# Second attention of a two-layer encoder: four units' softmax denominators turned at once, sent through DRAM and applied three units later

## The chip, the cores and the metric

The kernel is one program on one NeuronCore of a Trainium2 chip. The core has TensorE (PE in the profile: matmuls and transposes, results in PSUM), VectorE (DVE), ScalarE (ACT), GpSimd (POOL) and SyncE (SP, which here only issues transfers). Each engine works through its own instructions in order and waits on semaphore counts for what others produce. PSUM has eight banks of 128 partitions by 512 float32 words. The metric is the device time in microseconds of one execution. Before the change it was 1394.36 us, the median of three runs (1393.14 to 1395.08).

## What is computed

The reference is a two-layer encoder on a sequence of 1024 positions with 1024 features in float32. Layer 0 mixes tokens by a dilated window attention, layer 1 by a latent attention with 16 heads of width 64, and each layer ends in a gated residual and a layer norm. The change lies in layer 1's attention:

```python
s = (jnp.einsum('bqhd,bkhd->bhqk', qn, k_nope)
     + jnp.einsum('bqhd,bkd->bhqk', qr, k_rope)).astype(jnp.float32) * scale
p = jax.nn.softmax(s, axis=-1).astype(v.dtype)
return jnp.einsum('bhqk,bkhd->bqhd', p, v)
...
y = o * jax.nn.silu(gate)
return y @ w_out
```

For each head, every query row of 1024 scores is exponentiated and divided by its sum (the denominator), multiplied with the values, and the result is multiplied with a gate. Because the gate multiplies the same rows, the division may be made on the gate instead of on the probabilities, before or after the gate has met the attention output.

## The kernel before

Every float32 operand of a large matmul is split into a high and a low part of type float32r, and three matmuls (high by high, low by high, high by low; lines L89 to L91) replace one.

Layer 1's attention is `layer_b_attention`. It runs over 128 units u: 16 heads times 8 blocks of 128 queries. The parts of a unit are spread over several turns of the loop:

- `front(u)`: six matmuls of 128x512 into a scores tile `s` (two banks, two buffers).
- `soft(u)`: VectorE takes the row maximum (L1251). `expo(u)`: ScalarE's exponential with the row sum as a by-product (L1257).
- `middle(u)`, two turns later: eight PE transposes of the probabilities `pr` (L1270) into two one-bank tiles `t`; ScalarE casts each to the high part `pth` (L1273) and VectorE subtracts for the low part `ptl` (L1274); VectorE takes the reciprocal of the row sum (L1275), GpSimd spreads it over 64 columns of a tile `den` (L1276). The even and the odd unit share the tiles.
- `back(w)`, every second turn, for the pair of units w: one PE transpose of `den` (L1285) into columns 256 to 383 of a one-bank tile `o`; sixteen matmuls of 128x256 into columns 0 to 255 of the same bank (L1293, "the value matmuls" below); two ScalarE copies out of it (L1298, L1299); VectorE multiplies the turned reciprocals with the gate (L1302); GpSimd adds the two halves and multiplies with that product into the gate tile `gT` (L1305, L1306).

The one-bank tiles (`t`, `o`, and `m` of the projections) rotate through four banks; the scores take the other four.

Between the units two generators, `b_turn` and `b_qk`, prepare the queries and keys of the next two heads with the up-projection weights `wuh`/`wul`, which `b_weights` loads (SyncE) and splits (ScalarE L1110, GpSimd L1111), once in 16 units; `b_v` makes the values of four heads once in 32 units.

TensorE and SyncE run in the order in which the code is written. The orders of ScalarE, VectorE and GpSimd are set by a scheduler when the program is built, so for these the place of a line in the code is not its place in the queue; the built program tells it. All three wait in order: an instruction that is not ready holds everything behind it.

## Time and profile before

| | |
|---|---|
| median of three runs | 1394.36 us |
| profiled execution | 1399.57 us, its span 1397.8 us |
| second attention | from 817 to 1308 us of the span |
| PE busy in the span | 1355.3 us (97%) |
| DVE, ACT, POOL busy in the span | 938.9 (67%), 820.3 (59%), 573.6 us (41%) |

A row of a group reads: line, engine, operation, tile written <- tiles read, shape, xcount, then busy time in us and mean ns of one, then the idle time of that engine just before these instructions and what ended it. In a row of a timeline stand start, duration (both us from the span's start), engine, line, operation, shapes; rows next to each other of the same kind are merged with their count. In a row of a table by stretches stand the stretch, its length, the busy time and count of PE, PEld (weight loads), DVE, ACT and POOL, then the granted share of the TensorE clock, the share of the transfer engines and GB/s. PE's busy time is that of pipelined matmuls whose ends are modelled: a matmul shown with 0.28 us starts 0.12 us after the one before.

### The profile page before, as it was taken

Reading aid. Unit: us, or ns where it says so; the run is one execution under the profiler, and the core shown is the slowest. Engines: PE = TensorE matmul, PEld = TensorE weight load, DVE = VectorE, ACT = ScalarE, POOL = GpSimd, SP = SyncE. Lnnn points to the kernel's source line nnn. Section 1 sums busy time; section 2 is a strip of 40 time slices with the busy share of each in tenths; the row PEclk is TensorE's granted clock in tenths of the full one; section 3 lists DMA queues with packets and bytes.
Section 4 is the critical chain, followed back from the end, with each engine's and each line's share of the span. In section 5 each row is a group of like instructions: output and inputs, shape, how many; then the busy total and the mean of one; then the engine's idle time right before and its main releaser. Section 6 shows DMA issues by size and latency. Waiting matters only on the chain.

```text
span 1397.8 us, 21019 instructions
## 1 busy us (share of the span) xinstructions
PE 1355.3 (97%) x7523; PEld 1160.8 (83%) x7523; DVE 938.9 (67%) x1708; ACT 820.3 (59%) x1604; POOL 573.6 (41%) x657
## 2 busy tenths in 40 slices
PE   6999999999999999999999999999999999999897
PEld 5788888888888788888987888888889888898786
DVE  7654354555455492746745178898988889888787
ACT  3575565565443452425752178788787878888321
POOL 5341233132122226903742254634463463444653
PEclk9999999999999999999999999999999999999999
DMA  9422211022244302544145001010010100014132
GB/s 356 112 64 36 59 50 50 25 60 73 95 151 123 99 31 77 180 149 151 61 119 166 21 14 37 16 30 16 22 29 18 35 16 16 16 61 133 49 113 83
DMA packets 39721, 105.26 MB, mean 75 GB/s; under 512 B 5126, under 2 KB 11270, under 8 KB 39617
## 3 DMA queue, kind: packets, MB, share of 16 engines
q1 hardware_dynamic: 35608, 91.80, 21.3%
q0 software_dynamic: 3552, 12.06, 3.5%
q8 instruction: 60, 0.98, 0.3%
q14 instruction: 45, 0.36, 0.1%
q10 hardware_dynamic: 456, 0.05, 0.0%
HBM read 87.60 MB, written 8.43 MB: 69 GB/s over the span
## 4 chain that ended last, share of the span: by engine, by line
PE 74%; DVE 12%; ACT 5%; issue 4%; DMA 4%; SPq 0%; POOL 0%; DVEq 0%; ACTq 0%
PE pj L89 7%; PE pj L91 7%; PE pj L90 7%; PE o L1293 5%; PE t L1270 5%; PE po L89 4%; PE po L91 4%; PE po L90 4%; DVE mb L1251 3%; PE s L91 3%; PE s L89 3%; PE s L90 3%; PE pg L89 2%; PE pg L90 2%; PE pg L91 2%
## 5 line engine op out<-in xcount | busy, mean ns | idle before, releaser
L89 PE MATMUL pj<-uh,wh 128*128 128x512 f32 x528 | 216.0, 409 | 0.0
L91 PE MATMUL pj<-uh,wl 128*128 128x512 f32 x528 | 207.4, 393 | 0.0
L90 PE MATMUL pj<-ul,wh 128*128 128x512 f32 x528 | 207.4, 393 | 0.0
L1274 DVE TENSOR_TENSOR ptl<-t,pth 128x512 fp32r<-128x512 f32 x256 | 165.4, 682 | 3.0 <-ACT pth L1273 0.9
L1251 DVE TENSOR_REDUCE mb<-s 128x1 f32<-128x1024 f32 x128 | 155.8, 1217 | 7.9 <-PE s L91 6.3
L1257 ACT ACTIVATE pr<-s,mb 128x1024 f32<-128x1024 f32 x128 | 143.4, 1120 | 29.2 <-DVE mb L1251 21.1
L1273 ACT CAST pth<-t 128x512 fp32r<-128x512 f32 x256 | 138.9, 589 | 36.2 <-PE t L1270 34.1
L102 POOL TENSOR_TENSOR wl<-wraw,wh 128x1024 fp32r<-128x1024 f32 x43 | 106.6, 2485 | 106.7 <-ACT wh L101 54.6
L1270 PEld LDWEIGHTS t<-ident,pr 128*128 128x128 f32 x1024 | 119.3, 140 | 19.7 <-DVE ptl L1274 2.6
L1270 PE MATMUL t<-ident,pr 128*128 128x128 f32 x1024 | 133.2, 272 | 1.9 <-DVE ptl L1274 1.9
L1293 PE MATMUL o<-pth,vq 128*128 128x256 f32 x512 | 130.4, 292 | 0.0
L1293 PE MATMUL o<-ptl,vq 128*128 128x256 f32 x512 | 125.5, 283 | 0.8 <-DVE ptl L1274 0.8
L507 ACT ACTIVATE sb<-sb,stat 128x256 f32<-128x256 f32 (+1 forms) x144 | 67.0, 467 | 98.6 <-DVE stat L501 98.5
L91 PEld LDWEIGHTS pj<-uh,wl 128*128 128x128 f32 x528 | 99.4, 188 | 22.2
L1276 POOL COPY den<-mb 128x64 f32<-128x64 f32 x128 | 30.1, 236 | 203.2 <-DVE mb L1275 193.6
L90 PEld LDWEIGHTS pj<-ul,wh 128*128 128x128 f32 x528 | 100.1, 190 | 14.3
L89 PEld LDWEIGHTS pj<-uh,wh 128*128 128x128 f32 x528 | 99.9, 189 | 14.5
L89 PE MATMUL s<-kb,q 128*128 128x512 f32 x256 | 104.4, 408 | 0.2 <-ACT pr L1257 0.2
L91 PE MATMUL s<-kb,q 128*128 128x512 f32 x256 | 101.3, 396 | 0.0
L90 PE MATMUL s<-kb,q 128*128 128x512 f32 x256 | 100.8, 394 | 0.0
L1293 PEld LDWEIGHTS o<-ptl,vq 128*128 128x128 f32 x512 | 97.7, 191 | 1.4 <-DVE ptl L1274 1.4
L1293 PEld LDWEIGHTS o<-pth,vq 128*128 128x128 f32 x512 | 97.7, 191 | 0.2
(288 smaller groups left out, 3317.6 us busy)
## 6 DMA issues: line engine op xcount, KB each, us to landing
wraw<-wa SPq DMA_DIRECT2D x36, 512.0 KB, 4.9
ada<-ada_row SPq DMA_DIRECT2D x64, 256.0 KB, 3.6
wraw<-wo_a SPq DMA_DIRECT2D x18, 512.0 KB, 3.6
ada<-ada_ss SPq DMA_DIRECT2D x16, 512.0 KB, 8.2
kb<-kb POOLq DMA_DIRECT2D x30, 256.0 KB, 3.4
xc<-xt SPq DMA_DIRECT2D x8, 512.0 KB, 9.2
xr<-x SPq DMA_DIRECT2D x8, 512.0 KB, 5.7
xn_d<-z POOLq DMA_DIRECT2D x8, 512.0 KB, 4.6
```

What stands on the lines that cost most here:

```text
L89: mm(out, wh, xh, start=start, stop=False)
L90: mm(out, wh, xl, start=False, stop=False)
L91: mm(out, wl, xh, start=False, stop=stop)
L102: (lo_engine or self.nc.gpsimd).tensor_tensor(l[:, :width], raw[:, :width], f32(h[:, :width]), op=ALU.subtract)
L507: nc.scalar.activation(sb[:, a * w : a * w + w], sb[:, a * w : a * w + w], AF.Exp, bias=stat[:, 0, hh, t : t + 1], scale=-1.0, accum_out=s ...
L1251: nc.vector.tensor_reduce(m[:, 0:1], s, axis=AX.X, op=ALU.max, negate=True)
L1257: nc.scalar.activation(pr, s, AF.Exp, bias=m[:, 0:1], accum_out=m[:, 1:2])
L1270: nc.tensor.transpose(pt[:, c * P : c * P + P], pr[:, kt * P : kt * P + P], self.ident)
L1273: nc.scalar.copy(h, src)
L1274: nc.vector.tensor_tensor(l, src, f32(h), op=ALU.subtract)
L1276: nc.gpsimd.tensor_copy(st["den"][:, 64 * a : 64 * a + 64], m[:, 2:3].to_broadcast([P, 64]))
L1293: nc.tensor.matmul(po[:, 0:256], v, pts[j][x][:, c * 256 : c * 256 + 256], start=n == 0, stop=n == 15)
```

## The change

1. The row sums of eight units (one head) go into one small tile `den` of 128x8. After every fourth unit VectorE takes four reciprocals in one instruction (now L1278).
2. `spread(v)`, once for four units at the start of every second `back`: PE transposes the 128x4 reciprocals into partitions 0 to 3, columns 256 to 383 of the bank `o` of that `back` (L1285); ScalarE copies these 4x128 into a tile `rden` (L1289); SyncE writes them to a DRAM buffer `den_d` (L1290) and reads them back as one row of 512 repeated over 64 partitions (L1291).
3. `normalise(v)`, three turns later: GpSimd multiplies the 64x512 of the gate tile with `rden` (L1297).
4. In `back` the transpose of `den`, VectorE's two multiplications and the column range they used are gone. GpSimd multiplies the sum of the halves straight into the gate.
5. `b_wload` is split off `b_weights`: the raw up-projection weights are loaded one pair of heads (16 units) earlier, into the same buffers.
6. Two tables of the stage before move into the buffers that `rden` later uses.

```diff
     def b_weights(self, p):
-        raw = BS.tile([P, 640], F32, tag="wuraw", bufs=1, name=self.nm("wuraw"))
+        raw, rv, n = self.wuraw.pop(p)
...
+        self.b_wload(p + 1)
...
         def expo(u):
             s, m = st[u]
+            if u % 8 == 0:
+                dens[u // 8] = self.M.tile([P, 8], F32, tag="den", bufs=3, name=self.nm("den"))
             pr = self.ht(F32, "pr")
-            nc.scalar.activation(pr, s, AF.Exp, bias=m[:, 0:1], accum_out=m[:, 1:2])
-            st[u] = (pr, m)
+            nc.scalar.activation(pr, s, AF.Exp, bias=m[:, 0:1], accum_out=dens[u // 8][:, u % 8 : u % 8 + 1])
+            st[u] = pr
+            if u % 4 == 3:
+                d = dens[u // 8][:, u % 8 - 3 : u % 8 + 1]
+                nc.vector.reciprocal(d, d)
+
+        def spread(v, bank):
+            hd = v // 2
+            d = dens[hd][:, 4 * (v % 2) : 4 * (v % 2) + 4]
+            nc.tensor.transpose(bank[0:4, 256:384], d, self.ident)
+            t = rden[v] = self.M.tile([P, 512], F32, tag="rden", bufs=2, name=self.nm("rden"))
+            mine, other = slice(64 * (hd % 2), 64 * (hd % 2) + 64), 64 - 64 * (hd % 2)
+            rows = t[other : other + 4, 0:P]
+            nc.scalar.copy(rows, bank[0:4, 256:384])
+            nc.sync.dma_start(den_d[v].rearrange("(a b) -> a b", b=P), rows)
+            nc.sync.dma_start(t[mine, :], den_d[v : v + 1, :].to_broadcast([64, 512]))
+
+        def normalise(v):
+            hd = v // 2
+            mine = slice(64 * (hd % 2), 64 * (hd % 2) + 64)
+            g = self.gT[hd // 2][mine, v % 2 * 512 : v % 2 * 512 + 512]
+            nc.gpsimd.tensor_tensor(g, g, rden.pop(v)[mine, :], op=ALU.mult)
...
-            nc.vector.reciprocal(m[:, 2:3], m[:, 1:2])
-            nc.gpsimd.tensor_copy(st["den"][:, 64 * a : 64 * a + 64], m[:, 2:3].to_broadcast([P, 64]))
...
             po = self.PB.tile([P, 512], F32, tag="t", bufs=4, name=self.nm("o"))
-            nc.tensor.transpose(po[:, 256:384], den, self.ident)
+            if w % 2 == 0:
+                spread(w // 2, po)
...
             nc.scalar.copy(w3[mine, 0:256], po[other, 0:256])
-            nc.scalar.copy(w3[mine, 512:768], po[mine, 0:256])
-            for a in range(2):
-                qs = slice(a * P, a * P + P)
-                nc.vector.tensor_tensor(
-                    w3[mine, 256 + a * P : 384 + a * P], po[64 * a : 64 * a + 64, 256:384], g[:, qs], op=ALU.mult
-                )
-            nc.gpsimd.tensor_tensor(w3[mine, 0:256], w3[mine, 512:768], w3[mine, 0:256], op=ALU.add)
-            nc.gpsimd.tensor_tensor(g, w3[mine, 0:256], w3[mine, 256:512], op=ALU.mult)
+            nc.scalar.copy(w3[mine, 256:512], po[mine, 0:256])
+            nc.gpsimd.tensor_tensor(w3[mine, 0:256], w3[mine, 256:512], w3[mine, 0:256], op=ALU.add)
+            nc.gpsimd.tensor_tensor(g, w3[mine, 0:256], g, op=ALU.mult)
...
             if u >= 4 and u % 2 == 0 and u < nu + 4:
                 back((u - 4) // 2)
+            if u >= 7 and u % 4 == 3:
+                normalise((u - 7) // 4)
```

How the built orders move, at turn 56 (the fourteenth spread, v = 13; k = 55 is the last of its four units). Tile names carry buffer numbers. TensorE first, before, with what each row waits for:

```order
L91 MATMUL s_9414<-kb_5490,q_8703 128x512
L1270 MATMUL t_9428<-ident,pr_9360 128x128 [waits DVE_49]
L1270 MATMUL t_9428<-ident,pr_9360 128x128 x3
L1270 MATMUL t_9435<-ident,pr_9360 128x128 [waits DVE_49,PE_49,Activation_49]
L1270 MATMUL t_9435<-ident,pr_9360 128x128 x3
L1285 MATMUL o_9446<-ident,den_9343 128x128 [waits DVE_49,Pool_49]
L1293 MATMUL o_9446<-pth_9339,vq_8408 128x256 [waits Activation_49]
L1293 MATMUL o_9446<-ptl_9340,vq_8408 128x256
```

and with the change:

```order
L91 MATMUL s_9303<-kb_5490,q_8628 128x512
L1308 MATMUL t_9316<-ident,pr_9252 128x128 [waits DVE_49]
L1308 MATMUL t_9316<-ident,pr_9252 128x128 x3
L1308 MATMUL t_9323<-ident,pr_9252 128x128 [waits PE_49,Activation_49]
L1308 MATMUL t_9323<-ident,pr_9252 128x128 x3
L1285 MATMUL o_9333<-ident,den_8968 4x128 [waits DVE_49,PE_49]
L1330 MATMUL o_9333<-pth_9234,vq_8342 128x256 [waits Activation_49]
L1330 MATMUL o_9333<-ptl_9235,vq_8342 128x256
```

The rows stand in the same places. What the counts stand for differs: following each wait to the instruction that raises the count so far, the first value matmul of all 64 `back`s waited before for the cast of its own `pth`, made several units earlier; with the change that of every second `back` (32 of 64) waits for the copy L1289 out of the same bank. The transpose L1285 waited before for GpSimd's `den`; now it waits for VectorE's reciprocal L1278.

ScalarE at the same turn, before:

```order
L1273 CAST pth_9423<-t_9428 128x4x128
L1273 CAST pth_9425<-t_9435 128x4x128
L1257 ACTIVATE pr_9444,mb_9421<-s_9414,mb_9421 128x1024
L1201 ACTIVATE q_9471<-ab_9201 64x512
L1201 ACTIVATE q_9471<-ab_9244 64x512
L1298 COPY osum_9464<-o_9446 64x256
L1299 COPY osum_9464<-o_9446 64x256
```

and with the change:

```order
L1311 CAST pth_9312<-t_9316 128x4x128
L1311 CAST pth_9314<-t_9323 128x4x128
L1274 ACTIVATE pr_9331,den_9330<-s_9303,mb_9310 128x1024
L1215 ACTIVATE q_9360<-ab_9099 64x512
L1215 ACTIVATE q_9360<-ab_9142 64x512
L1289 COPY rden_9335<-o_9333 4x128
L1335 COPY osum_9355<-o_9333 64x256
L1336 COPY osum_9355<-o_9333 64x256
```

The copy L1289 stands behind both casts of the transposes just made, behind the exponential of unit 56 and, at this turn, behind two copies of the next head's queries. At the 32 spreads the rows just ahead of L1289 are of a few kinds, which but for the first and the last four come back every eight spreads: casts, exponential (v = 12, 15, 19 and their like); casts, exponential, two query copies (13, 17); weight split, two key casts, one cast (14, 18); two value casts, weight split, one cast (16).

VectorE with the change:

```order
L1266 TENSOR_REDUCE mb_9283<-s_9276 128x1
L1312 TENSOR_TENSOR ptl_9235<-t_9285,pth_9234 128x4x128
L1312 TENSOR_TENSOR ptl_9237<-t_9292,pth_9236 128x4x128
L1266 TENSOR_REDUCE mb_9310<-s_9303 128x1
L1278 RECIPROCAL den_8968<-den_8968 128x4
L1312 TENSOR_TENSOR ptl_9313<-t_9316,pth_9312 128x4x128
```

The four reciprocals, the last of them of unit 55, stand behind the row maximum of unit 56. Before, the reciprocal of unit 55 stood after the low parts that here follow it.

## The prediction

> **What bounds the kernel now.** I read the head of the page, then the attention's stretch in the table by stretches, then what PE waits for inside it.

> ```profile
> span 1397.8 us, 21019 instructions
> ...
> 817.00:1308.00 491.00, 485.36 (x3182) 430.71 (x3180) 428.68 (x744) 399.89 (x765) 224.53 (x348) 1.00 0.14 36
> ...
> PE m L89 <- DVE kb L1222: 2.4, 7, 0.4
> PE t L1270 <- DVE ptl L1274: 1.9, 3, 0.6
> ```

> PE works 485.4 of the attention's 491.0 us at full clock, so 5.6 us is all that removed waits can return; the two largest are shown. DVE (428.7 us) and ACT (399.9 us) run close behind but are not the bound. So an edit counts by what it does to PE: work taken from it, and waits put before it.

> **What is removed and what is hidden.** The groups of the same stretch:

> ```profile
> L1302 DVE TENSOR_TENSOR osum<-o,gT 64x128 f32<-64x128 f32 x128 | 36.8, 288 | 35.5 <-ACT osum L1299 31.6 <-PE s L90 1.2 <-POOL den L1276 0.6
> L1276 POOL COPY den<-mb 128x64 f32<-128x64 f32 x128 | 30.1, 236 | 203.2 <-DVE mb L1275 193.6 <-PE t L1270 6.9 <-PE o L1293 2.4
> L1257 ACT ACTIVATION_READ_ACCUMULATOR pr<-s,mb 128x1 f32 x128 | 25.4, 198 | 0.0
> L1298 ACT COPY osum<-o 64x256 f32<-64x256 f32 x64 | 23.5, 367 | 4.4 <-PE o L1293 3.1
> L1203 POOL TENSOR_TENSOR q<-rope,q 64x512 fp32r<-64x512 f32 x16 | 20.3, 1291 | 1.5 <-ACT q L1201 1.2
> L1275 DVE RECIPROCAL mb<-mb 128x1 f32<-128x1 f32 x128 | 20.0, 156 | 6.5 <-ACT pr L1257 3.7
> ```

> DVE loses 128 multiplications (36.8 us) and 128 reciprocals (20.0 us) and gets 32 reciprocals of four columns, at the 0.156 us of one column 5 us: 52 us less, on an engine that is not the bound. POOL loses 30.1 us of copies and gets 32 multiplications of 64x512; by the 1.291 us of L1203 that is 41 us, covered by its idle 266 us (491 less 224.5). ACT gets 32 copies of 4x128, each between its smallest row (0.198 us) and the 64x256 copy (0.367 us); I take 0.2 us, 6 us in all. PE loses 32 transposes; the other 32 still stream 128 columns and stay as they are.

> The transfers: from the spread to its use lie three units, 3 x 491/128 = 11.5 us.

> ```profile
> bias<-lines_d SPq DMA_DIRECT2D x30, 128.0 KB, 4.8
> wvraw<-wv SPq DMA_DIRECT2D x4, 128.0 KB, 2.9
> ...
>   DMA wuraw<-wu_e: 7.9, 1
> ```

> From DRAM, 128 KB land in 2.9 to 4.8 us; write and read after each other make 5.8 to 9.6 us, inside the 11.5. Meanwhile SP is held between the two, with weight loads queued behind that have 11 us (output weights) or more to go. Were the cover gone, POOL would wait for the difference, 0 to some 2 us a spread, out of its idle time; its multiplication has no PE instruction behind it that is due sooner than two spreads on. The earlier weight loads gain nothing: the only wait for such a load in the whole trace (7.9 us of ACT, once) lies before the attention. There SP is now held behind the first split until POOL has read the raw tile, about 5 us, and the gate weights queued behind are needed a whole gate block later. I take 0 for all of this, and 0 to 5 us as the range.

> **The new wait.** The orders ahead show that in 32 of 64 `back`s the first value matmul waits for the copy L1289, and that this copy stands in ACT's queue behind work which starts only when PE's last transposes are done. So PE, which now goes from the transposes straight on, has to wait for ACT to work off that queue. The rows before show when ACT gets there. Turn 56, the kind with two query copies:

> ```profile
> 1023.56 1.03 PE L1270 MATMUL t<-ident,pr 128*128 128x128 f32 x8
> 1024.43 0.27 PE L1285 MATMUL o<-ident,den 128*128 128x128 f32 x1
> 1024.46 0.36 PE L1293 MATMUL o<-pth,vq 128*128 128x256 f32 x1
> 1024.20 1.08 ACT L1273 CAST pth<-t 128x512 fp32r<-128x512 f32 x2
> 1025.28 1.11 ACT L1257 ACTIVATE pr<-s,mb 128x1024 f32<-128x1024 f32 x1
> 1026.51 1.15 ACT L1201 ACTIVATE q<-ab 64x512 fp32r<-64x512 f32 x2
> ```

> Eight transposes in 0.87 us make 0.11 us each: 32 of them off PE are -3.5 us. The value matmuls start at 1024.46; ACT ends its query copies at 1027.66. With 0.2 us for the copy and a hand-over of 0.1 us, PE stands 3.2 + 0.3 = 3.5 us. The other kinds (turns 64, 60, 52 and 68):

> ```profile
> 1055.37 1.21 DVE L1251 TENSOR_REDUCE mb<-s 128x1 f32<-128x1024 f32 x1
> 1055.49 0.36 PE L1293 MATMUL o<-pth,vq 128*128 128x256 f32 x1
> 1056.69 1.12 ACT L1257 ACTIVATE pr<-s,mb 128x1024 f32<-128x1024 f32 x1 [0.30 <-DVE mb L1275]
> 1057.92 0.36 ACT L1298 COPY osum<-o 64x256 f32<-64x256 f32 x1
> ...
> 1042.36 0.36 PE L1293 MATMUL o<-pth,vq 128*128 128x256 f32 x1
> 1042.91 0.59 ACT L1273 CAST pth<-t 128x512 fp32r<-128x512 f32 x1
> ...
> 1009.64 0.36 PE L1293 MATMUL o<-pth,vq 128*128 128x256 f32 x1
> 1013.53 1.11 ACT L1257 ACTIVATE pr<-s,mb 128x1024 f32<-128x1024 f32 x1 [3.15 <-DVE mb L1251]
> 1014.75 0.37 ACT L1298 COPY osum<-o 64x256 f32<-64x256 f32 x1
> ...
> 1071.38 1.07 ACT L1273 CAST pth<-t 128x512 fp32r<-128x512 f32 x2 [0.32 <-PE t L1270]
> 1071.59 0.36 PE L1293 MATMUL o<-pth,vq 128*128 128x256 f32 x1
> ```

> The hand-over is read here: DVE's maximum ends at 1056.58, ACT's exponential starts 0.11 us later. Casts and exponential: 1057.9 - 1055.5 + 0.3 = 2.7 us. One cast: 1043.5 - 1042.4 + 0.3 = 1.4 us. Turn 52, where DVE is behind with the rotary products and the exponential comes late: 1014.7 - 1009.6 + 0.3 = 5.4 us. Turn 68, where only the first of two casts stands ahead: 0.7 us. The reciprocal itself, behind a maximum that ends 1.1 us after PE is there (turn 64), is ready before ACT's queue is, so it adds nothing. Eight spreads as they come (5.4, 3.5, 1.4, 2.7, 0.7, 3.5, 1.4, 2.7) make 21.3 us, 32 make 85 us.

> These lags hold some backlog of DVE and ACT, which a standing PE lets them work off. The bound from below takes none: the first cast starts with the first four transposes done, so casts and exponential lead to 2.2 us, the query copies to 3.3, one cast to 1.0, turn 68 to 0.5; 15.7 us in eight, 63 us in all. In between I take 80 us, near the rows, since inside the three units that decide little is left to work off but turn 52's. While PE stands, its few other waits go too; I take 4 of the 5.6 us.

> [...]

> **The clock.** Stalls of this length do something else in the trace:

> ```profile
> 436.31:439.72 3.41, 1.86 (x10) 1.13 (x9) 0.00 (x0) 2.20 (x6) 1.03 (x1) 1.00 0.14 49
> 473.86:477.27 3.41, 1.28 (x9) 0.86 (x7) 1.51 (x6) 1.08 (x5) 0.00 (x0) 1.00 0.28 112
> 477.27:480.68 3.41, 3.41 (x12) 2.83 (x12) 0.42 (x1) 1.95 (x2) 0.00 (x0) 0.50 0.00 0
> 1316.95:1320.36 3.41, 1.03 (x5) 0.53 (x3) 2.74 (x2) 1.23 (x2) 3.41 (x2) 1.00 0.00 0
> 1320.36:1327.19 6.83, 6.22 (x15) 4.87 (x16) 6.13 (x5) 1.26 (x2) 6.83 (x3) 0.50 0.00 0
> ...
> 40.36:43.78 3.42, 1.60 (x10) 1.10 (x9) 3.32 (x3) 0.42 (x3) 2.75 (x3) 1.00 0.07 26
> 43.78:47.19 3.41, 3.41 (x10) 2.42 (x9) 3.19 (x6) 2.89 (x3) 1.10 (x1) 0.50 0.00 0
> ```

> The granted clock changes on a grid of 3.41 us. Stretches of it in which PE was busy 1.03, 1.28 and 1.60 us were followed by one or two at half clock; one with 1.86 us was not. So a stretch with PE idle for more than half (1.7 us) costs the next one half its speed, up to 1.7 us of work; part of that stretch can itself be stall, so I take 1.3. A stall placed at random against the grid fills half a stretch with a chance of its length over 3.41, once above 1.7. The modelled ends and the transpose keep PE busy for 0.4 us of each stall: 3.5 gives 0.9, 2.7 gives 0.67, 5.4 gives 1, the short ones 0. That is 4.1 drops in eight spreads, 16 in all, 21 us; the bounds are 0 and 20 drops of 1.7 us, 34 us.

> [...]

> **The sum:** 1397.8 + 80 - 3.5 - 4 + 21 = 1491 us of span. The span before lies 3.4 us above the median of the runs, so the forecast is 1488 us.

> **The rivals.**

> *The clock mostly holds.* The stalls come as above but are broken up by the transpose in their midst so that few stretches are half empty: 1397.8 + 75 - 7.5 + 3 - 3.4, about 1464 us. For it: the stretch with 1.55 us of idle that cost nothing. Against it: three that did.

> *The way through memory is late.* If a write to DRAM takes much longer to land than any row here, more than the 11.5 us, POOL waits and its key transfers and query parts behind come late to PE. Each us beyond the cover costs up to 32 us; from 12.5 us on the time is above 1520. No row of this size speaks for it.

> *It is faster.* DVE is what ACT's exponential waits for, and DVE is relieved by 52 us; if this pulled ACT so far forward that the copy is done when PE comes, the transposes and PE's idle time are won: 1394.4 - 3.5 - 5.6 = 1385 us. It would decide once ACT's lag of 1.1 to 3.2 us is gone. Against it: in the rows of turn 56 ACT does not wait for DVE at all, and its casts cannot start before the transposes that PE has just made.

> *It does not matter.* If stalls and gains came out equal, within 3 us of 1394; it would need stalls of 0.3 us a spread, which only turn 68 comes near.

> **How the numbers follow.** Forecast with its clock drops 0.60, the clock holds 0.24, late memory 0.08, faster 0.05, no difference 0.03. A measurement of this kernel can tell 0.2% from no change. Faster 0.05, same 0.03, slower 0.92. The low end takes the stalls at their bound with few drops, 1397.8 + 63 - 9 - 3.4 = 1448, less some margin 1440; the high end 85 us of stalls and 34 us of drops, 1510, and with the 5 us of hidden work and some second stretches at half clock 1520. What is left out holds 0.16 and the tails.

> **What will show it.** Right: PE's first value matmul waits 32 times for ACT's copy, in sum 60 to 90 us; DVE's busy time in the attention falls to about 377 us; the granted clock in the attention falls to about 0.9. Wrong: PE busy in more than nine tenths of the attention; a copy that stands ready before PE's transposes; waits of PE that lead to GpSimd or a transfer.

## The result, and the profile after

| | before | changed | ratio, 95% interval |
|---|---|---|---|
| median of four runs each, same chip | 1393.75 us | 1483.82 us | 1.0643, 1.0631 to 1.0655 |
| range | 1392.95 to 1395.08 | 1483.44 to 1485.69 | |
| span of the profiled execution | 1397.8 us | 1483.3 us | |
| first to last scores matmul of the second attention | 473.3 us | 562.4 us | |

The changed kernel is 90 us slower; 1488 us was forecast, 1440 to 1520 the range. The last line of the table, read from the start times of PE's scores matmuls in the two traces, says where: the second attention takes 89.1 us more. (The two profiled spans differ by 85.5 us only, because the profiled execution of before was a long one, 1399.6 us against the median of 1393.75; it reached the attention at 813.8 us, the changed kernel at 809.6.)

The attention of the changed kernel in the table by stretches (us, then busy time of PE, PEld, DVE, ACT and POOL with counts, granted clock, DMA share, GB/s):

```profile
812.00:1395.00 583.00, 515.96 (x3160) 450.43 (x3159) 385.54 (x522) 407.28 (x801) 236.16 (x252) 0.95 0.13 38
```

The stretch that took 491 us takes 583. PE, which had 5.6 us idle there, has 67, and the time in which it counts as busy has itself grown from 485 to 516 us at a clock of 0.95: much the same matmuls, some of them at a granted clock of 0.50 (the stretches below). DVE is 43 us lighter (428.7 to 385.5), as the edit intends, and the time does not fall for it.

What PE waits for in this stretch, from the list of waits (us in total, times, longest):

```profile
PE o L1330 <- ACT rden L1289: 41.1, 32, 2.2
PE o L1285 <- DVE den L1278: 24.2, 21, 3.9
PE m L89 <- DVE kb L1236: 1.6, 7, 0.2
```

The groups of the new or changed instructions there:

```profile
L1330 PE MATMUL o<-pth,vq 128*128 128x256 f32 x512 | 147.8, 320 | 41.1 <-ACT rden L1289 41.1
L1297 POOL TENSOR_TENSOR gT<-gT,rden 64x512 f32<-64x512 f32 x31 | 39.6, 1276 | 2.4
L1289 ACT COPY rden<-o 4x128 f32<-4x128 f32 x32 | 7.8, 245 | 3.0 <-issue 2.8
L1278 DVE RECIPROCAL den<-den 128x4 f32<-128x4 f32 x32 | 5.4, 169 | 1.2 <-ACT pr L1274 1.2
```

Two waits stand where there were none. In all 32 spreads the first value matmul waits for ScalarE's copy; in 21 the small transpose ahead of it waits for VectorE's reciprocal as well. The list counts from the modelled end of the instruction before; counted by PE's pace (start to start, less the 0.11 us that a transpose takes when nothing holds it) the 32 spreads stand 27.8 us for the reciprocal and 46.5 us for the copy, 74.3 us together. The multiplication on GpSimd costs what its row of before said (1.28 us each) and nobody waits for it.

Turn 56 of the changed kernel, which the prediction showed before the change: PE's rows, then ScalarE's, then VectorE's, from the timeline.

```profile
1059.51 1.03 PE L1308 MATMUL t<-ident,pr 128*128 128x128 f32 x8
1061.21 0.27 PE L1285 MATMUL o<-ident,den 128*4 128x128 f32 x1 [0.67 <-DVE den L1278]
1063.68 0.58 PE L1330 MATMUL o<-pth,vq 128*128 128x256 f32 x1 [2.20 <-ACT rden L1289]
...
1060.14 1.07 ACT L1311 CAST pth<-t 128x512 fp32r<-128x512 f32 x2
1061.10 1.13 ACT L1274 ACTIVATE pr<-s,mb 128x1024 f32<-128x1024 f32 x1
1062.11 0.21 ACT L1274 ACTIVATION_READ_ACCUMULATOR pr<-s,mb 128x1 f32 x1
1062.34 1.14 ACT L1215 ACTIVATE q<-ab 64x512 fp32r<-64x512 f32 x2
1063.39 0.24 ACT L1289 COPY rden<-o 4x128 f32<-4x128 f32 x1
...
1059.77 1.21 DVE L1266 TENSOR_REDUCE mb<-s 128x1 f32<-128x1024 f32 x1
1060.90 0.17 DVE L1278 RECIPROCAL den<-den 128x4 f32<-128x4 f32 x1
```

ScalarE works without a gap: casts, exponential, two query copies, then the copy. PE has issued its last transpose at 1060.3 and starts the value matmuls at 1063.68, 0.05 us after the copy's end. What the reciprocal adds inside this (0.83 us by pace) is hidden behind ScalarE's queue: had the transpose come earlier, ScalarE would still reach the copy only at 1063.39, 2.2 us after it.

Four stretches on the clock's grid of the changed kernel, in two pairs:

```profile
1060.28:1063.69 3.41, 0.55 (x5) 0.12 (x3) 1.96 (x4) 3.33 (x7) 0.47 (x1) 1.00 0.24 49
1063.69:1067.10 3.41, 3.41 (x16) 3.41 (x17) 0.00 (x0) 0.00 (x0) 0.00 (x0) 0.50 0.12 39
...
1166.10:1169.51 3.41, 1.81 (x14) 1.62 (x15) 1.61 (x4) 1.81 (x5) 0.12 (x1) 1.00 0.14 29
1169.51:1172.92 3.41, 3.41 (x23) 3.00 (x22) 1.35 (x2) 1.65 (x4) 1.46 (x2) 1.00 0.28 96
```

PE busy for 0.55 of 3.41 us: the next stretch runs at half clock, with 16 PE instructions in it against 23 in the full stretch of the other pair. PE busy for 1.81: the next runs at full clock. In the attention 13 such drops came, 18 stretches at half clock in all.

### The profile page after: what moved, and what is told of

Its sections match the earlier page's. It is cut to its first block, busy times and chain, and to the rows that moved or that the text cites. A ratio compares the mean times of both kernels' runs of the same rounds, so it can differ in the third digit from the quotient of the medians.

```text
span 1483.3 us, 20543 instructions
## 1 busy us (share of the span) xinstructions
PE 1379.2 (93%) x7491; PEld 1175.0 (79%) x7491; DVE 894.2 (60%) x1484; ACT 825.4 (56%) x1636; POOL 585.5 (39%) x561
## 3 DMA queue, kind: packets, MB, share of 16 engines
q1 hardware_dynamic: 38424, 96.07, 20.5%
## 4 chain that ended last, share of the span: by engine, by line
PE 66%; DVE 15%; ACT 8%; issue 6%; DMA 4%; SPq 0%; POOL 0%; DVEq 0%; ACTq 0%; POOLq 0%
PE o L1330 9%; PE pj L89 7%; PE pj L90 7%; PE pj L91 7%; DVE mb L1266 4%; PE t L1308 3%; PE s L89 3%; PE s L90 3%; PE s L91 3%; PE po L89 2%; PE po L91 2%; PE po L90 2%; DMA ada<-ada_row 2%; DVE ptl L1312 2%; PE o L556 2%
## 5 line engine op out<-in xcount | busy, mean ns | idle before, releaser
L89 PE MATMUL pj<-uh,wh 128*128 128x512 f32 x528 | 215.5, 408 | 0.0
L90 PE MATMUL pj<-ul,wh 128*128 128x512 f32 x528 | 207.0, 392 | 0.0
L1330 PE MATMUL o<-pth,vq 128*128 128x256 f32 x512 | 147.8, 320 | 41.1 <-ACT rden L1289 41.1
L1337 POOL TENSOR_TENSOR osum<-osum 64x256 f32<-64x256 f32 x64 | 47.4, 740 | 294.6 <-ACT osum L1336 294.4
L1274 ACT ACTIVATE pr<-s,mb 128x1024 f32<-128x1024 f32 x128 | 144.3, 1127 | 13.5 <-DVE mb L1266 13.1
L1330 PEld LDWEIGHTS o<-pth,vq 128*128 128x128 f32 x512 | 110.2, 215 | 49.3 <-ACT rden L1289 49.3
L1330 PE MATMUL o<-ptl,vq 128*128 128x256 f32 x512 | 140.8, 306 | 0.0
L89 PEld LDWEIGHTS pj<-uh,wh 128*128 128x128 f32 x528 | 99.7, 189 | 14.4
L90 PEld LDWEIGHTS pj<-ul,wh 128*128 128x128 f32 x528 | 99.8, 189 | 14.1
L1330 PEld LDWEIGHTS o<-ptl,vq 128*128 128x128 f32 x512 | 110.8, 216 | 0.0
L89 PE MATMUL s<-kb,q 128*128 128x512 f32 x256 | 106.2, 415 | 0.1
L90 PE MATMUL s<-kb,q 128*128 128x512 f32 x256 | 102.5, 401 | 0.0
L91 PE MATMUL s<-kb,q 128*128 128x512 f32 x256 | 101.7, 397 | 0.0
```

The lines of the kernel that those rows point to most:

```text
L89: mm(out, wh, xh, start=start, stop=False)
L90: mm(out, wh, xl, start=False, stop=False)
L91: mm(out, wl, xh, start=False, stop=stop)
L1274: nc.scalar.activation(pr, s, AF.Exp, bias=m[:, 0:1], accum_out=dens[u // 8][:, u % 8 : u % 8 + 1])
L1330: nc.tensor.matmul(po[:, 0:256], v, pts[j][x][:, c * 256 : c * 256 + 256], start=n == 0, stop=n == 15)
L1337: nc.gpsimd.tensor_tensor(w3[mine, 0:256], w3[mine, 256:512], w3[mine, 0:256], op=ALU.add)
```

## The experiments

The theory: the whole loss is PE standing ahead of the value matmuls, for the reciprocal and for ScalarE to come to the copy, and the clock that these stalls cost; the way through memory, GpSimd's multiplication and the earlier loads cost nothing. "On the same chip" below means beside runs of the kernel before in the same series.

### The spread behind the value matmuls

```diff
-            if w % 2 == 0:
-                spread(w // 2, po)
             hq = hd % 4
...
                         nc.tensor.matmul(po[:, 0:256], v, pts[j][x][:, c * 256 : c * 256 + 256], start=n == 0, stop=n == 15)
                         n += 1
+            if w % 2 == 0:
+                spread(w // 2, po)
```

> The spread (reciprocal, transpose, copy, both transfers) is written behind the sixteen value matmuls of the same `back`, not ahead of them; all else is as in the change. Theory (the loss is PE standing ahead of the value matmuls, for the reciprocal and then for ScalarE's copy, plus the clock that these stalls cost): no value matmul waits for the copy, the 46.5 us of waits for the copy are gone, of the 27.8 us for the reciprocal at most 3 x 2 us are left (the turn-52 kind, whose reciprocal is ready about 5 us after PE is there, against 2 us of value matmuls), no clock drop but a few; 1483.8 - 74 - 20 = about 1390 us, range 1382 to 1400. Rival 1 (the way through memory or GpSimd's long multiplication costs something by itself): it stays above 1410, with waits of PE that lead to GpSimd or to a transfer. Rival 2 (the relief of VectorE and the 32 transposes fewer were worth more than the 3.5 us and 4 us of the sum): below 1382.

Measured: 1397.6 us against 1395.2 on the same chip, ratio 1.0015 (1.0000 to 1.0030). Moving one call by sixteen matmuls takes back all but 2.4 us of the 90, and the interval hardly tells these from nothing. PE's waits in the attention:

```profile
PE o L1285 <- DVE den L1278: 5.6, 3, 1.9
PE m L89 <- DVE kb L1236: 2.4, 7, 0.3
```

No wait for the copy, and three for the reciprocal of the turn-52 kind, as expected; two of the three were followed by a stretch at half clock, the only ones in this attention. The transfers, the DRAM buffer and GpSimd's multiplications are all still there, so they are not the loss. The relief of VectorE is still there too and does not show: rival 2 falls.

The same place in the odd `back`, by which time the reciprocals have long been ready (the diff is against the variant above):

```diff
-            if w % 2 == 0:
+            if w % 2 == 1:
                 spread(w // 2, po)
...
-            if u >= 7 and u % 4 == 3:
-                normalise((u - 7) // 4)
+            if u >= 9 and u % 4 == 1:
+                normalise((u - 9) // 4)
...
+        normalise(31)
```

> The spread is written behind the value matmuls of the odd `back`, two turns later than in the change, and the multiplication two turns later too (the last one after the loop). Theory: the reciprocal's operands are long there when the transpose comes, and nothing of PE waits for the copy; so the transposes of the spread wait for nothing, and what is left against the kernel before is 32 transposes fewer (-3.5 us) and a few of the 5.6 us of idle time: 1393.8 - 3.5 - 0 to 4 = 1386 to 1391 us, a little under the variant with the spread behind the value matmuls of the even `back`. Rival (multiplication on GpSimd or the path by DRAM holds something up): above 1395, with a wait of PE behind GpSimd.

Measured: 1394.9 us, ratio 0.9996 (0.9987 to 1.0006): the 1386 to 1391 us of the theory were missed, and no wait of PE behind GpSimd speaks for the rival. The attention took 468.9 us (before 473.3), 4.4 us less, within what was expected of the whole; but the stretch from there to the end of the span grew from 110.6 to 113.3 us. That is taken up below.

### Which of the two waits is worth what

A PSUM tile of its own for the turned reciprocals; the value matmuls then write another bank:

```diff
-                spread(w // 2, po)
+                spread(w // 2, self.mbank("sd"))
```

> The spread's transpose goes into a PSUM tile of its own instead of columns 256 to 383 of the bank in which the value matmuls then sum, so the value matmuls do not have to wait for ScalarE's copy; place and order of the spread stay as in the change, so PE still stands at the transpose until the reciprocal is there. Theory: the 46.5 us of waits for the copy are gone, the 27.8 us for the reciprocal stay or grow a little (PE is early more often, since it is no longer held at the copy): 25 to 40 us; clock drops, 13 in the change, fall to the four or so of the turn-52 kind: about 1483.8 - 46.5 - 12 = 1425 us, range 1410 to 1440. Rival (the wait for the copy only covers another one, for instance VectorE's reciprocal queue or the casts, which then takes its place): above 1455.

Measured: 1429.6 us, ratio 1.0248 (1.0233 to 1.0264). Turn 56 in its timeline, PE then ScalarE:

```profile
1039.06 0.27 PE L1285 MATMUL sd<-ident,den 128*4 128x128 f32 x1 [0.67 <-DVE den L1278]
1039.08 0.36 PE L1330 MATMUL o<-pth,vq 128*128 128x256 f32 x1
...
1041.24 0.24 ACT L1289 COPY rden<-sd 4x128 f32<-4x128 f32 x1
```

The value matmuls start 2.2 us before the copy: with another bank nothing ties them to it here. In 22 of 32 spreads it is so; in ten (the turn-60 and turn-68 kinds) the first value matmul still goes on only behind the copy, 8.9 us in sum. Why the built program keeps that wait there is open. By pace the stalls are 36.8 us, 27.9 of them for the reciprocal, the clock drops are three (13 in the change), and the attention is 32.7 us longer than before.

The opposite: the transpose stays in the value matmuls' bank and ahead of them, so that they wait for the copy, but in the odd `back`, when the reciprocals have long been ready (the diff is against the change).

```diff
-            if w % 2 == 0:
+            if w % 2 == 1:
                 spread(w // 2, po)
             hq = hd % 4
...
-            if u >= 7 and u % 4 == 3:
-                normalise((u - 7) // 4)
+            if u >= 9 and u % 4 == 1:
+                normalise((u - 9) // 4)
...
+        normalise(31)
```

> The spread ahead of the value matmuls as in the change, but of the odd `back`, two turns later, with the multiplication two turns later too. The reciprocals are then ready long before PE comes to the transpose; the first value matmul still waits for ScalarE's copy, which stands behind an exponential and a cast. Theory (two waits add up in the change: 27.8 us for the reciprocal and 46.5 us for ScalarE to come to the copy): the wait at the spread's transpose is 0 instead of 27.8 us, the wait at the first value matmul is 1.2 to 2.4 us a spread, 40 to 75 us in all, and the time 1430 to 1480 us, never back to 1395. Rival (it is the late reciprocal alone that makes ScalarE's copy late): the copy's wait shrinks below 15 us, time below 1415.

Measured: 1415.6 us in one run (before 1394.0 on the same chip). Both sides missed: the wait for the reciprocal is gone as the theory said (0.2 us by pace), but the wait for the copy fell to 27.7 us, less than the theory's 40 and more than the rival's 15. PE and ScalarE in a long case of this kernel:

```profile
1036.42 0.27 PE L1285 MATMUL o<-ident,den 128*4 128x128 f32 x1
1038.35 0.39 PE L1330 MATMUL o<-pth,vq 128*128 128x256 f32 x1 [1.65 <-ACT rden L1289]
...
1035.61 1.12 ACT L1274 ACTIVATE pr<-s,mb 128x1024 f32<-128x1024 f32 x1
1036.62 0.19 ACT L1274 ACTIVATION_READ_ACCUMULATOR pr<-s,mb 128x1 f32 x1
1036.83 0.58 ACT L1234 CAST kb<-m 64x512 fp32r<-64x512 f32 x1
1037.43 0.58 ACT L1311 CAST pth<-t 128x512 fp32r<-128x512 f32 x1
1038.04 0.25 ACT L1289 COPY rden<-o 4x128 f32<-4x128 f32 x1
```

Most of the other spreads in it stand 0.5 us: one cast, the copy, two hand-overs. ScalarE's queue in the odd turns is another one and mostly shorter, so the 46.5 us do not belong to the copy as such but to what the change's own turns put ahead of it. That a late reciprocal lengthens the wait for the copy by itself is not shown, since the turn moved with it.

The copy on VectorE in place of ScalarE:

```diff
-            nc.scalar.copy(rows, bank[0:4, 256:384])
+            nc.vector.tensor_copy(rows, bank[0:4, 256:384])
```

> The change with the spread's copy on VectorE in place of ScalarE. There the copy stands behind the maximum, the reciprocal and both low parts of the same turn, which wait for ScalarE's casts of PE's last transposes. Theory (any engine with work behind the last transposes ahead of the copy stalls PE): the wait at the transpose stays near 28 us and the wait at the first value matmul is about the low parts' lag, 1 to 2 us a spread, 32 to 64 us; time 1455 to 1490 us. Rival (it is ScalarE's load of exponentials and query copies): the wait for the copy is under 0.5 us a spread, time below 1435.

Measured: 1476.6 us in one run. By pace 27.7 us for the reciprocal and 39.2 us, 1.2 us a spread, for the copy, which on VectorE stands behind the low parts. The theory holds: it is the place behind the last transposes' work that costs, on either engine.

### What the clock takes

```diff
+            one, two = FILLS.get(v, {0: (0, 0), 1: (7, 14), 2: (0, 0), 3: (7, 5)}[v % 4])
+            for _ in range(one):
+                nc.tensor.transpose(bank[:, 384:512], self.ident, self.ident)
             nc.tensor.transpose(bank[0:4, 256:384], d, self.ident)
+            for _ in range(two):
+                nc.tensor.transpose(bank[:, 384:512], self.ident, self.ident)
```

(`FILLS` holds the pairs of the long and the last kinds.)

> The change with dummy transposes of the identity into columns 384 to 511 of the same bank, which nothing reads, ahead of and behind the spread's transpose, in numbers that fill the stalls seen in its trace (7 to 35 ahead, 5 to 14 behind, by kind of turn). What the value matmuls wait for stays the same; only PE is busy while it waits. Theory (the stalls cost by themselves 74 us, and a further 20 us through the granted clock): the clock in the attention holds, at most three drops, the waits of the first value matmul for the copy fall since the time is filled, and the time falls to 1483.8 - 20 = about 1464 us, range 1457 to 1472. Rival (the clock drops fall into time in which PE waits anyway and cost nothing): no faster than 1480, or slower by what the dummies overshoot.

Measured: 1463.4 us, ratio 1.0490 (1.0473 to 1.0508). Its attention in the table by stretches:

```profile
813.00:1370.00 557.00, 532.93 (x3572) 472.32 (x3571) 383.15 (x520) 404.20 (x797) 233.94 (x251) 1.00 0.13 38
```

Its list of waits (lines six further down than in the change):

```profile
PE o L1336 <- ACT rden L1295: 22.5, 32, 1.3
```

With 420 more instructions on PE the kernel is 20 us faster than the change, and the clock of the attention is 1.00: no stretch of it at half speed. The stalls are still there, some two thirds of them filled. So the clock's share is 20.5 us by the medians (of two series), 23.5 us by the attention alone (562.38 to 538.85).

### A version that beats both, and the earlier loads

In the variant with the spread behind the value matmuls of the odd `back`, the last multiplication came two turns later as well. Here the last two spreads go behind the even `back` (the diff is against that variant):

```diff
-            if w % 2 == 1:
+            if (w % 2 == 1 and w < 60) or w in (60, 62):
                 spread(w // 2, po)
...
-            if u >= 9 and u % 4 == 1:
+            if u >= 9 and u % 4 == 1 and u < 128:
                 normalise((u - 9) // 4)
+            if u in (127, 131):
+                normalise((u - 7) // 4)
...
-        normalise(31)
```

> As the variant with the spread behind the value matmuls of the odd `back`, but the last two spreads are put behind the value matmuls of the even `back` (as in the first variant), so that the last multiplications end before the output projection begins. That variant's attention, first to last scores matmul, took 468.9 us against 473.3 us of the kernel before, but the stretch from there to the end of the span took 113.3 against 110.6 us. Theory (the late multiplication at the end gave the gain back): attention 469 us, the rest about 110.5 us, time 1395.2 - 4.4 = about 1391 us, range 1388 to 1394. Rival (the end of the span differs from run to run and has nothing to do with the last multiplication): no difference that can be told from the kernel before, 1393.5 to 1397.

Measured: 1391.3 us against 1394.0, ratio 0.9981 (0.9972 to 0.9990): the only version below the kernel before, by 2.7 us. Its attention takes 469.5 us, the rest to the end of the span 110.3: the end is short again. The same kernel once more, in another series:

> The same variant with the earlier loads once more, on the chip on which its twin without them runs, so that the two stand beside each other. Theory: 2 to 4 us under the kernel before, and within 1.5 us of its twin. Rival (early loads cost): 1.7 us above its twin.

Measured: 1393.1 against 1394.7 us, ratio 0.9986 (0.9975 to 0.9996): again under the kernel before, but by 1.6 us, not the 2 to 4 expected. Its twin without the second part of the change:

```diff
-        raw, rv, n = self.wuraw.pop(p)
+        raw = BS.tile([P, 640], F32, tag="wuraw", bufs=1, name=self.nm("wuraw"))
+        n = 384 if p % 2 else 640
+        nc.sync.dma_start(raw[:, 0:n], A["wu_o" if p % 2 else "wu_e"][p // 2])
...
-        self.b_wload(p + 1)
```

> The variant with the spread behind the value matmuls of the odd `back` (the last two of the even), without the earlier loads. Theory (the early loads are worth nothing): 1391.3 us within 1.5 us, as with them. Rival (the early loads cost the 1.7 us seen when they stood alone): about 1389.6 us, 0.3% under the kernel before.

Measured: 1401.5 us, ratio 1.0051 (1.0032 to 1.0071), 8.4 us above the variant with the earlier loads in the same series. Neither the theory nor the rival had it: here the earlier loads are worth something. SyncE's queue and then ScalarE, in the timeline of the twin (lines 13 less than in the change):

```profile
862.04 0.24 SPq L1277 DMA_DIRECT2D den_d<-rden  x1
863.32 0.45 SPq L1278 DMA_DIRECT2D rden<-den_d  x1
863.86 0.54 SPq L1110 DMA_DIRECT2D wuraw<-wu_e  x1
...
868.96 0.74 ACT L1111 ACTIVATE wuh<-wuraw 128x640 fp32r<-128x640 f32 x1 [2.53 <-DMA wuraw<-wu_e]
```

The load stands in SyncE's queue behind the spread, whose write waits for ScalarE's copy, and leaves only when the spread is through. Six times in the attention ScalarE then waits 2.3 to 3.0 us for raw weights (15.8 us in sum, and none with the earlier loads); PE's waits for ScalarE's and VectorE's part of a unit (scores, transposes, value matmuls) come to 6.7 us, against 3.2, and the attention is 6.6 us longer (475.8 against 469.2). The loads a pair ahead leave from the same place in the queue, behind a spread (in the version with them 863.76 us for the read, 864.30 for the load), but that tile is split only at 913.41, 49 us later, so nobody waits.

In the change itself, with the same edit:

> The change with its second part undone: the up-projection weights are loaded again when they are split, not a pair ahead. Theory (the loads are worth nothing either way): 1483.8 us within 3 us, and no wait of PE behind a weight load. Rival (the earlier load costs the 1.7 us that the kernel before with this part alone took more, 1395.7 against 1394.0 us): about 1482 us, with the difference ahead of the attention or in its first turns. A third way (GpSimd and VectorE, now busier around the spreads, need the weights early): above 1487 us.

Measured: 1485.4 us, ratio 1.0661 (1.0643 to 1.0679), against 1.0643 for the change: not to be told apart. ScalarE waits there too for raw weights (11.5 us in the attention), and it does not show in the time; that PE's longer stalls cover it is the likely reason, not one that was tested by itself. And the earlier loads alone, the same lines added to the kernel before:

> The kernel before with the second part of the change alone: up-projection weights loaded a pair ahead. Theory (their loads are nowhere what PE waits for): same as before, 1395.2 us within 0.2%. Rival (a load a pair ahead takes room or memory bandwidth from others, or saves a wait): more than 3 us off in one direction, with a wait of PE or ScalarE behind a weight load to show for it.

Measured: 1395.7 against 1394.0 us, ratio 1.0016 (1.0006 to 1.0025). A small loss, inside the theory's 0.2% though the interval sets it apart from nothing; the rival's 3 us are not reached. Its attention takes 473.7 us (before 473.3) and its list of waits is the same, so where the 1.7 us lie is open.

## Why the prediction was right

The forecast was right in its size and in its mechanism. Term by term:

| term | predicted | measured |
|---|---|---|
| stalls ahead of the value matmuls | 80 us (63 to 85) | 74.3 us |
| 32 transposes fewer | -3.5 us | not measured apart |
| PE's other waits in the attention | -4 us | -3.9 us (5.5 to 1.6) |
| clock | 21 us (0 to 34) | 20.5 to 23.5 us |
| sum | 93.5 us | 87 to 90 us with -3.5; medians 90.1 us |

*The new wait.* One sign was missed: the value matmuls' wait for the copy was to come to 60 to 90 us, and it is 41.1 us by the list, 46.5 by pace. The rest of the 74.3 us PE stands one instruction earlier, at the transpose, for the reciprocal. By kind of turn, in the order of the prediction (52, 56, 60, 64, 68): 5.4, 3.5, 1.4, 2.7 and 0.7 us were predicted; 5.2, 3.2, 1.2 to 1.5, 2.0 and 0.6 us came. Mis-sized is the turn-64 kind: its 2.7 us held a backlog that the standing PE lets VectorE and ScalarE work off, which the prediction had named and booked on turn 52. There it was wrong: turn 52 keeps its full stall, because four rotary products (2.8 us) stand between the low parts and the maximum on VectorE. The other kinds came out near the bound from below (3.3, 1.0, 2.2 and 0.5), so the 80 us, taken near the rows, were on the high side. PE, then VectorE, at turn 52:

```profile
1039.02 1.04 PE L1308 MATMUL t<-ident,pr 128*128 128x128 f32 x8
1043.95 0.37 PE L1285 MATMUL o<-ident,den 128*4 128x128 f32 x1 [3.89 <-DVE den L1278]
1045.24 0.58 PE L1330 MATMUL o<-pth,vq 128*128 128x256 f32 x1 [0.92 <-ACT rden L1289]
...
1039.53 0.67 DVE L1182 TENSOR_TENSOR ab<-m,cs 64x512 f32<-64x512 f32 x1
...
1041.64 0.69 DVE L1183 TENSOR_TENSOR ab<-m,cs 64x512 f32<-64x512 f32 x1
1042.37 1.23 DVE L1266 TENSOR_REDUCE mb<-s 128x1 f32<-128x1024 f32 x1
1043.62 0.18 DVE L1278 RECIPROCAL den<-den 128x4 f32<-128x4 f32 x1
```

*The reciprocal "adds nothing".* True of the sum where ScalarE's queue lasts longer, as at turn 56, but it hid that the reciprocal is a wait of its own: with the copy out of the way (own bank) 27.9 us of stall were left. That variant got back 54 of the 90 us, not all of them.

*The bank.* With a tile of its own the value matmuls of turn 56 start 2.2 us ahead of the copy, and 22 of the 32 spreads have no wait for it; in the shared bank all 32 wait (41.1 us by the list). Why the built program waits was not shown; ten waits (8.9 us) stay with a bank of its own.

*The clock.* 16 drops of 1.3 us were predicted; 13 came, but five of them lasted two stretches, so the price of a drop was 1.6 to 1.8 us. The term came out right by two errors that cancel, which is luck. The clock of the stretch is 0.95 where about 0.9 was forecast, and PE's busy share, 516 of 583 us, stays just under the nine tenths above which the forecast would have been wrong. The rival in which the clock holds (1464 us; its terms add up to 1464.9) is what the filled stalls gave by hand: 1463.4 us.

*Hidden work.* The multiplication on GpSimd (1.28 us, 1.291 predicted), the copy (0.245 us, 0.2 predicted) and VectorE's relief (43 us in the table by stretches where 52 were forecast, 385.5 us left in place of 377) moved nothing. The way through memory was put at 5.8 to 9.6 us and is shorter: in the version that beats both, GpSimd waits for it (27 times, 40.0 us of its idle time), and from the end of the copy (967.98 + 0.25) to the multiplication it is 4.1 us. ScalarE's and GpSimd's rows there:

```profile
967.98 0.25 ACT L1289 COPY rden<-o 4x128 f32<-4x128 f32 x1
...
972.34 1.29 POOL L1297 TENSOR_TENSOR gT<-gT,rden 64x512 f32<-64x512 f32 x1 [1.71 <-DMA rden<-den_d]
```

*The earlier loads at nothing.* Right for the change as it stands, and probably for a reason that the prediction did not give: PE's stalls cover them, while without the stalls (the twin) their lack cost 8.4 us. It had seen that SyncE is held between write and read with weight loads behind, and asked only about loads that the change puts early; loads left in their old place would have been the ones to suffer.

## What to carry to other kernels

Here a small result that shared a PSUM bank with a large accumulation made TensorE wait for the queue of the engine that reads the small result (32 waits, 41.1 us by the list), and with the transpose behind the accumulation that wait was gone (1397.6 us in place of 1483.8). So put such a transpose behind the accumulation in the instruction order, two turns later if its input is late, and price it by the other engine's backlog at that point (2.2 us at turn 56), not by the 0.25 us of the copy. The 43 us taken from VectorE, which was not the bound, did not show in the time; TensorE was the bound, and the 74.3 us for which it stood did show, with 20.5 to 23.5 us more for the clock, which was granted at 0.50 after the stretches of its 3.41 us grid in which PE was idle for 55% or more. The round trip through DRAM held what was queued behind it on SyncE's transfer queue (in the twin ScalarE waited 15.8 us for raw weights, six times), so what is queued there has to be issued well ahead of its use (here 16 units ahead, and no such wait).

## What the runs showed of the hardware

```profile
1194.37:1197.78 3.41, 1.60 (x12) 1.32 (x12) 2.09 (x5) 3.02 (x6) 0.35 (x1) 1.00 0.23 47
1197.78:1201.20 3.42, 3.42 (x13) 3.00 (x12) 0.00 (x0) 0.73 (x2) 0.89 (x2) 0.50 0.14 43
```

A single stall of 2.05 us by pace (the spread behind the even value matmuls) cost the clock in two of three places, and stalls of 2.0 us in the change (turn 64 and its like) in none of seven. So the length of a stall did not tell alone; that it matters where the stall falls on the grid is the likely reason, not one that was tested by itself.

And idle TensorE time was filled at a gain: with 420 transposes that compute nothing, run while TensorE had to wait, the kernel took 1463.4 us in place of 1483.8, and the clock of the attention was 1.00 in place of 0.95. The stretch at 1170.18 us there, in which 31 of these transposes start, was followed by full clock.
